# First MLP product of a transformer block on TensorE: plain blocks of features, or seven half-size products per four blocks

## The chip, the cores and the metric

The kernel runs on one core of one Trainium2 chip. The metric is device microseconds of one execution. Matrix products run on TensorE (PE in the profile; PEld is its weight loading), element-wise work on VectorE (DVE), ScalarE (ACT) and GpSimd (POOL). Transfers are issued from queues, mostly SyncE's (SP); those that add onto their destination are issued from GpSimd's queue.

## The reference

One block: a normalization, an input projection, two attention branches, an output projection, and an MLP with a squared ReLU; sequence 512, width 1024, hidden width 4096, all in float32. What the change touches is the MLP line:

```python
    h = h + merged @ w_out[l]
    m = rmsnorm(h, g_mlp[l])
    h = h + jnp.square(jax.nn.relu(m @ w_ff1[l])) @ w_ff2[l]
return rmsnorm(h, g_final)
```

## The kernel before

Every float32 operand is split into a high and a low part, and a product is three matmuls: high by high, high by low, low by high (mm3, lines 87 to 90). A split is one ScalarE pass (the high part) and one VectorE subtraction (split, lines 92 to 94).

The MLP runs in four quarters of eight blocks of 128 hidden features. For each block, hidden loads a weight slice of 1024 x 128 (one DMA of 512 KB), splits it, and multiplies it with the normalized tokens: 8 steps of depth x 3 matmuls = 24 matmuls with 512 tokens as the moving operand. ScalarE evicts the result with a ReLU, and two squares sort its token halves into px and qx. A pair of blocks (pair_units) so gives one 2 x 2 arrangement: rows are token halves, columns are feature blocks.

The second product of a quarter is already done by the seven-product scheme (Strassen-Winograd): the blocks of the second weight, B11 to B22, are combined by add_w2 on VectorE (line 988), the left sides by left_sums on VectorE, and block_product runs seven products of 24 matmuls each, with 512 output columns. prep splits the weights of a product two products ahead; ORDER is the sequence. add_rows (line 1427) adds each result to the rows of h, which live in SBUF to the end. The last products and the final normalization are in last_rows.

Blocks 0 and 1 of the first quarter are multiplied earlier, in two halves of 256 tokens while the rows are still being normalized (early, f00 and f01). The output projection before the MLP uses the same scheme; there load_onto adds pairs of weight blocks by DMA from GpSimd's queue (line 984), and merged_sums forms some left sums on GpSimd.

SBUF tiles come from pools by tag: u2 has 29 buffers of 128 x 512, u4 has 26 of 128 x 2 x 512, wf has 3 weight landings, wh and wl have 4 split weights each. A new tile waits until a buffer of its tag is free. in_program_order pins the order of instructions on chosen engines as they are written; a transfer on SP's queue goes when its buffer is free and its turn comes.

Of the kernel before, what the change touches and what calls it, by code (L numbers as in the profile page):

```python
# [11 lines left out]
F32 = mybir.dt.float32  # L12
# [6 lines left out]
P = 128  # L19
# [37 lines left out]
def tile_block(ctx: ExitStack, tc: tile.TileContext, t, out: bass.AP):  # L57
# [129 lines left out]
    class Flipped:  # L187
        def __init__(self, gains, name):
            self.gains, self.name = gains, name
            self.out = [u4(f"{name}T{k}") for k in range(KD)]  # L190
            self.banks = {}
# [11 lines left out]
        def evacuate(self, half, ks=range(KD)):  # L203
            tok = slice(half * 256, half * 256 + 256)
            for k in ks:
                hl = self.out[k]
                src = self.banks[half][k % 4][:, (k // 4) * 256 : (k // 4) * 256 + 256]
                split_scaled(hl[:, 0, tok], hl[:, 1, tok], src, self.gains[:, k : k + 1])
# [50 lines left out]
    R = one([P, S], F32, "R")  # L259
# [108 lines left out]

    def gated(acc, name):
# [3 lines left out]
        th = u2(f"t{name}")  # L373
        nc.scalar.activation(th, z, AF.Tanh, scale=0.5)  # L374
        return z, th
# [11 lines left out]
    g2 = [gated(f_accs[2 + x], f"b{x}")[1] for x in range(2)]  # L387
# [47 lines left out]
    class Gates:  # L435
# [20 lines left out]
        def sums(self, d):  # L456
            i = 0 if d == "f" else 1
            rr = tl([P, NT, P + 1], F32, "rr", 2, f"rr{d}")
# [469 lines left out]
    def left_sums(px, qx, name, eng):  # L928

        a11, a12, a21, a22 = px[:, 0:HT], px[:, HT:S], qx[:, 0:HT], qx[:, HT:S]  # L930
        y, z = u2(f"y{name}"), u2(f"z{name}")
        s1, s2, s3, s4 = y[:, 0:HT], y[:, HT:S], z[:, 0:HT], z[:, HT:S]
        eng.tensor_tensor(s1, a21, a22, op=ALU.add)
        eng.tensor_tensor(s2, s1, a11, op=ALU.subtract)  # L934
        eng.tensor_tensor(s3, a11, a21, op=ALU.subtract)
        eng.tensor_tensor(s4, a12, s2, op=ALU.subtract)
        return y, z

# [47 lines left out]
    def add_w2(dst, x, y, op):  # L986
        for g in range(NP // 2):
            nc.vector.tensor_tensor(wq[dst][g], wq[x][g], wq[y][g], op=op)  # L988

# [18 lines left out]
    def split_w2(x, name):  # L1008
        return [split_part(x, g, name) for g in range(NP // 2)]

    def merged_sums(p, eng):
        px, qx = merged[p]
        a11, a12, a21, a22 = px[:, 0:HT], px[:, HT:S], qx[:, 0:HT], qx[:, HT:S]
        y, z = u2(f"yo{p}"), u2(f"zo{p}")
# [154 lines left out]
    def finish_zb(f, begun):  # L1171
        g2.append(gated(proj_run(begun, xT), f"b{f}")[1])
# [147 lines left out]
    g2.append(gated(zb, "b6")[1])  # L1320
# [18 lines left out]
    g2.append(gated(proj_run(zb, xT, None, range(3, KD)), "b7")[1])  # L1339
# [108 lines left out]
    def prep(m, qd):  # L1448

        more = qd + 1 < NQ  # L1450
        name = f"b{m}_{qd}"
        if m == 1:
            return split_w2(B11, name)
        if m == 2:
            res = split_w2(B21, name)
            if more:
                load_w2(qd + 1, B21)
            return res
        if m == 3:
            return split_w2(B22, name)  # L1460
        if m == 5:
            add_w2(B11, B12, B11, ALU.subtract)
            return split_w2(B11, name)
        if m == 6:
            add_w2(B11, B22, B11, ALU.subtract)
            return split_w2(B11, name)
        if m == 7:
            add_w2(B12, B22, B12, ALU.subtract)
            res = split_w2(B12, name)
            if more:  # L1470
                load_w2(qd + 1, B12)
                load_w2(qd + 1, B22)
            return res
        add_w2(B11, B21, B11, ALU.subtract)
        res = split_w2(B11, name)
        if more:
            load_w2(qd + 1, B11)
        return res

    def hidden(qd, j):  # L1480

        if qd == 0 and j < 2:
            acc = early[j][2]
# [277 lines left out]
```

## Time and profile before

| | |
|---|---|
| time, median of 3 runs | 759.76 us (759.3 to 759.81) |
| profiled execution | 758.17 us |
| its span, first to last instruction | 756.5 us |
| instructions in the span | 10217 |
| moved by DMA | 81.30 MB, mean 107 GB/s |
| HBM read and written | 76.96 MB, 2.10 MB |

The profiled execution is one run of its own; its span is the time from its first to its last instruction, and what remains lies around it. A row of a group gives line, engine, operation, output and inputs, shapes and count, then busy time and the mean duration of one in ns, then the idle time of the engine just before them. [...]

### The profile page before, as it was taken

How to read it: one execution, taken by the hardware profiler on the slowest of the kernel's cores; microseconds unless marked ns; L12 is line 12 of the kernel's file. 1: busy time of each engine (PE TensorE's matmuls, PEld its weight loads, DVE VectorE, ACT ScalarE, POOL GpSimd, SP SyncE). 2: the span in 40 equal slices, each digit the busy share in tenths (PEclk: the TensorE clock that was granted, in tenths of full speed). 3: DMA queues.
4: the chain of work that ended last, by engine and by line, in shares of the span. 5: the costliest groups of instructions: out<-in, count | busy, mean ns of one | idle time of the engine just before them, and what ended most of it. 6: DMA issues, size and time to landing. Idle time of an engine off the chain costs nothing.

```text
span 756.5 us, 10217 instructions
## 1 busy us (share of the span) xinstructions
PE 745.2 (99%) x3704; PEld 629.7 (83%) x3704; DVE 592.5 (78%) x887; ACT 468.1 (62%) x812; POOL 128.1 (17%) x186
## 2 busy tenths in 40 slices
PE   8999999999999999999999999999999999999996
PEld 7888788888888888899988988888888888888885
DVE  7779899687787787998897787856696578748795
ACT  7556658478767576988866766345544555345644
POOL 1620002031321115036850100000000000000014
PEclk9999999999999999999999999999999999999998
DMA  9832311312234324237998411461126410650003
GB/s 316 255 95 91 128 29 28 84 49 62 59 84 112 60 50 112 73 89 184 273 203 221 133 57 55 139 193 58 56 61 203 127 56 3 206 154 0 29 0 112
DMA packets 97075, 81.30 MB, mean 107 GB/s; under 512 B 15376, under 2 KB 74784, under 8 KB 97024
## 3 DMA queue, kind: packets, MB, share of 16 engines
q1 hardware_dynamic: 93760, 74.07, 33.1%
q0 software_dynamic: 2976, 6.05, 4.3%
q8 instruction: 29, 0.48, 0.3%
q10 hardware_dynamic: 288, 0.52, 0.2%
q14 instruction: 22, 0.18, 0.1%
HBM read 76.96 MB, written 2.10 MB: 105 GB/s over the span
## 4 chain that ended last, share of the span: by engine, by line
PE 93%; ACT 2%; DVE 2%; issue 1%; DMA 1%; POOL 0%; POOLq 0%; ACTq 0%; DVEq 0%
PE f L89 8%; PE f L88 8%; PE f L90 8%; PE gx L88 4%; PE gx L89 4%; PE gx L90 4%; PE first L329 3%; PE tp L1116 2%; PE gz L89 2%; PE gz L88 2%; PE gz L90 2%; PE zb L88 1%; PE za L88 1%; PE zb L90 1%; PE za L90 1%; PE za L89 1%
## 5 line engine op out<-in xcount | busy, mean ns | idle before, releaser
L1700 POOL DMA_DIRECT2D gfin<-in_g_final x1 | 0.6, 623 | 284.1 <-PE f L90 284.1
L988 DVE TENSOR_TENSOR w<-w,w 128x1024 f32<-128x1024 f32 x32 | 38.7, 1219 | 0.3
L1101 ACT ACTIVATE e<-s,top 128x512 f32<-128x512 f32 x32 | 21.9, 685 | 4.4 <-DVE top L1096 3.5
L94 DVE TENSOR_TENSOR pT<-tp,pT 128x512 fp32r<-128x512 f32 x32 | 21.6, 681 | 2.9 <-ACT pT L93 2.9
L1096 DVE TENSOR_REDUCE top<-s 128x1 f32<-128x512 f32 x32 | 21.6, 680 | 2.0 <-PE s L90 1.7
L1427 DVE TENSOR_TENSOR h<-h,gx 128x512 f32<-128x512 f32 x32 | 21.4, 680 | 1.9 <-PE gx L90 1.8
L93 ACT ACTIVATE pT<-tp 128x512 fp32r<-128x512 f32 x32 | 18.8, 592 | 4.3 <-PE tp L1116 4.0
L479 POOL COPY v3f<-rrf 128x4 f32<-128x4 f32 x4 | 2.8, 705 | 109.3 <-DVE rrf L462 109.3
L1116 PE MATMUL tp<-ident,e 128*128 128x128 f32 x128 | 19.3, 274 | 0.3 <-ACT e L1107 0.2
L88 PE MATMUL av<-pT,v 128*128 128x256 f32 x64 | 19.0, 298 | 0.0
L93 ACT ACTIVATE ghb<-y 128x512 fp32r<-128x512 f32 x16 | 10.1, 632 | 14.0 <-DVE y L934 14.0
L1493 ACT ACTIVATE fa<-f 128x512 f32<-128x512 f32 x32 | 18.4, 576 | 0.0
L89 PE MATMUL av<-pT,v 128*128 128x256 f32 x64 | 18.2, 285 | 0.0
L90 PE MATMUL av<-pT,v 128*128 128x256 f32 x64 | 18.2, 284 | 0.0
L1116 PEld LDWEIGHTS tp<-ident,e 128*128 128x128 f32 x128 | 15.1, 140 | 3.7 <-ACT e L1107 1.0
L93 ACT ACTIVATE b_00h<-w 128x1024 fp32r<-128x1024 f32 x7 | 7.4, 1060 | 12.6 <-PE gz L90 6.0
L93 ACT ACTIVATE b_10h<-w 128x1024 fp32r<-128x1024 f32 x7 | 7.4, 1060 | 12.1 <-PE gz L90 6.0
L93 ACT ACTIVATE b_20h<-w 128x1024 fp32r<-128x1024 f32 x7 | 7.4, 1060 | 12.1 <-PE gz L90 6.0
L88 PE MATMUL s<-kbuf,q 96*128 96x512 f32 x32 | 14.1, 441 | 0.0
L374 ACT ACTIVATE tb<-zb 128x512 f32<-128x512 f32 x8 | 5.0, 632 | 14.7 <-DVE zb L372 14.7
L1502 ACT ACTIVATE px<-fa 128x256 f32<-128x256 f32 x32 | 13.4, 418 | 1.0
L984 POOL DMA_DIRECT2D w<-in_w_out x10 | 12.2, 1397 | 6.5 <-DVE bo60l L94 5.3
(1743 smaller groups left out, 2919.1 us busy)
## 6 DMA issues: line engine op xcount, KB each, us to landing
w<-in_w_ff SPq DMA_DIRECT2D x64, 256.0 KB, 3.4
w<-in_w_out POOLq DMA_DIRECT2D x10, 512.0 KB, 8.8
grw<-in_w_in SPq DMA_DIRECT2D x8, 512.0 KB, 9.1
gvw<-in_w_in SPq DMA_DIRECT2D x8, 512.0 KB, 4.5
w<-in_w_out SPq DMA_DIRECT2D x16, 256.0 KB, 5.9
x<-in_xt SPq DMA_DIRECT2D x8, 256.0 KB, 5.3
h<-in_x SPq DMA_DIRECT2D x4, 512.0 KB, 5.1
vw<-in_w_first SPq DMA_DIRECT2D x7, 256.0 KB, 5.4
```

What stands on the lines that cost most here:

```text
L88: nc.tensor.matmul(acc, lh, rh, start=start, stop=False, skip_group_check=onto)
L89: nc.tensor.matmul(acc, lh, rl, start=False, stop=False, skip_group_check=onto)
L90: nc.tensor.matmul(acc, ll, rh, start=False, stop=stop, skip_group_check=onto)
L93: nc.scalar.activation(hi, src, AF.Copy)
L94: rest.tensor_tensor(lo, src, raw(hi), op=ALU.subtract)
L329: nc.tensor.matmul(f_accs[i], a[:, i * P : (i + 1) * P], b, start=k == 0 and x == 0, stop=k == KD - 1 and x == 2)
L988: nc.vector.tensor_tensor(wq[dst][g], wq[x][g], wq[y][g], op=op)
L1096: nc.vector.tensor_reduce(top, acc, axis=AX.X, op=ALU.max, negate=True)
L1101: nc.scalar.activation(e, acc, AF.Exp, bias=top, accum_out=tot[:, qt % 2 : qt % 2 + 1])
L1116: nc.tensor.transpose(tp[:, k * P : (k + 1) * P], e[:, k * P : (k + 1) * P], ident)
L1427: nc.vector.tensor_tensor(hc, hc, acc, op=op)
L1493: nc.scalar.activation(a, acc, AF.Relu)
```

## The change

The first MLP product of blocks 4 to 31 is done by the seven-product scheme too. Four blocks of 128 features form a quad: the weight (1024 x 512) is cut into 2 x 2 blocks of 512 x 256, the normalized tokens into 2 x 2 blocks of depth half by token half. Each of the seven products is 2 feature blocks x 4 steps of depth x 3 = 24 matmuls with 256 tokens. Blocks 0 to 3 stay plain, now all in two token halves. There are seven quads; the first quarter has the four plain blocks and one quad, each later quarter two quads.

- The tokens' sums are formed once (m_sums: two of 128 x 1024 on GpSimd, six on VectorE) and split (m_split, four).
- Each quad needs two weight sums by DMA (load_first, then load_onto from GpSimd's queue) and two by GpSimd (in prep). Five plain loads of 512 KB and two adding ones replace four loads.
- In the second product add_w2 is gone: sums with B12 are adding DMAs, the others GpSimd additions (Group.onto). The left sums (summed_rows) move from VectorE to GpSimd, but for the plain pairs and part of the last.
- Weights are split run by run: a Step is half a second product or one product of a quad, and prepare splits up to two steps ahead; the second product's first steps are interleaved with the last products of the quad before. The order on PE, ScalarE, VectorE and GpSimd is pinned as written.
- u2 goes from 29 to 24 buffers, u4 from 26 to 30; tiles of the early stages (gates, scans, R) change tag.

```diff
-        return tl(list(shape), dt, "u2", 29, name)
+        return tl(list(shape), dt, "u2", 24, name)
-        return tl(list(shape), dt, "u4", 26, name)
+        return tl(list(shape), dt, "u4", 30, name)
...
-    def add_w2(dst, x, y, op):
-        for g in range(NP // 2):
-            nc.vector.tensor_tensor(wq[dst][g], wq[x][g], wq[y][g], op=op)
...
-    def pair_units(qd, p, a22):
-        px, qx = u2(f"px{qd}{p}"), u2(f"qx{qd}{p}")
-        for x in range(2):
-            a = hidden(qd, 2 * p + x)
-            c = slice(x * HT, (x + 1) * HT)
-            nc.scalar.activation(px[:, c], a[:, 0:HT], AF.Square)
-            nc.scalar.activation(qx[:, c], a[:, HT:S], AF.Square)
-        left = {}
-        split_first(left, px, f"{qd}{p}")
-        y, z = left_sums(px, qx, f"{qd}{p}", nc.vector)
-        split_sum(left, y, 5, 6, f"b{qd}{p}")
-        split_sum(left, z, 7, 3, f"c{qd}{p}")
-        split_corner(left, qx, a22, p)
-        return left
...
+    def left_rest(left, p, px, qx, a22, name, eng=nc.gpsimd, low=nc.vector):
+        y, z = summed_rows(px, qx, name, eng)
+        def rest(part=0):
+            if part < 2:
+                split_sum(left, y, 5, 6, f"b{name}", low)
+            if part != 1:
+                split_sum(left, z, 7, 3, f"c{name}", low)
+                split_corner(left, qx, a22, p)
+        return rest
...
+    def m_sums(c):
+        for j in range(2):
+            hi, lo = fm.out[j, c]
+            r = m_raw[j, c] = u4("mr", F32, (P, KD // 2, HT))
+            (nc.vector if c else nc.gpsimd).tensor_tensor(r, raw(hi), raw(lo), op=ALU.add)
+            if j == 0 and c == 1:
+                nc.vector.tensor_tensor(m_raw[0, 0], m_raw[0, 0], r, op=ALU.subtract)
+        if c == 0:
+            return
+        a, b, c, d = (m_raw[k] for k in ((0, 0), (1, 1), (0, 1), (1, 0)))
+        nc.vector.tensor_tensor(c, b, c, op=ALU.subtract)
+        nc.vector.tensor_tensor(b, b, a, op=ALU.add)
+        nc.vector.tensor_tensor(d, b, d, op=ALU.subtract)
+        m_of[1], m_of[2], m_of[3] = fm.out[0, 0], fm.out[1, 0], fm.out[1, 1]
+        m_raw.update({5: a, 6: b, 7: c, 4: d})
...
+    FIRST = (1, 5, 2, 6, 3, 7, 4)
+    class Quad:
+        def __init__(self, q):
+            self.q, self.ready = q, {}
+        def rows(self, i, j):
+            c = (4 * self.q + 2 * i) * P
+            return w1[j * S : (j + 1) * S, c : c + HT].rearrange("(k p) w -> p k w", p=P)
+        def load_first(self):
+            shape = (P, KD // 2, HT)
+            self.a, self.e = (u4(f"w1{x}{self.q}", F32, shape) for x in "ae")
+            for dst in (self.a, self.e):
+                nc.sync.dma_start(dst, self.rows(1, 0))
+        def load_onto(self):
+            for dst, other in ((self.a, (1, 1)), (self.e, (0, 0))):
+                nc.gpsimd.dma_start(dst, self.rows(*other), accum_op=ALU.add)
+        def load_sums(self):
+            self.load_first()
+            self.load_onto()
+        def load(self, x):
+            dst = stage(KD // 2, HT, f"w1{x}{self.q}")
+            nc.sync.dma_start(dst, self.rows(*{"b": (0, 0), "c": (0, 1), "d": (1, 1)}[x]))
+            setattr(self, x, dst)
+        def prep(self, m):
+            src = {1: "b", 5: "a", 2: "c", 6: "b", 3: "c", 7: "e", 4: "d"}[m]
+            wh, wl = halves(KD // 2, HT, f"w1{m}{self.q}")
+            split(wh, wl, getattr(self, src))
+            self.ready[m] = wh, wl
+            if m == 1:
+                nc.gpsimd.tensor_tensor(self.b, self.a, self.b, op=ALU.add)
+            elif m == 2:
+                nc.gpsimd.tensor_tensor(self.c, self.b, self.c, op=ALU.add)
+        def run(self, m):
+            bank = {1: "x", 5: "z", 2: "w", 6: "x", 3: "z", 7: "x", 4: "x"}[m]
+            begin = m in (1, 5, 2)
+            if begin:
+                setattr(self, bank, ps("mm", f"f{bank}{self.q}"))
+            acc = getattr(self, bank)
+            wh, wl = self.ready.pop(m)
+            hi, lo = m_of[m]
+            for x in range(2):
+                c = slice(x * HT, (x + 1) * HT)
+                f = slice(x * P, (x + 1) * P)
+                for k in range(KD // 2):
+                    mm3(acc[:, c], wh[:, k, f], wl[:, k, f], hi[:, k, :], lo[:, k, :],
+                        begin and x == 0 and k == 0, k == KD // 2 - 1, True)
+        def after(self, m):
+            q = self.q
+            if m == 1:
+                self.px = u2(f"px{q}0")
+                nc.scalar.activation(self.px, self.x, AF.Copy)
+            elif m == 5:
+                self.qy = u2(f"qx{q}1")
+                nc.scalar.activation(self.qy, self.z, AF.Copy)
+            elif m == 2:
+                nc.vector.tensor_tensor(self.px, self.w, self.px, op=ALU.add)
+            elif m == 6:
+                self.qx = u2(f"qx{q}0")
+                nc.scalar.activation(self.qx, self.x, AF.Copy)
+            elif m == 3:
+                nc.vector.tensor_tensor(self.qx, self.z, self.qx, op=ALU.add)
+            elif m == 7:
+                nc.vector.tensor_tensor(self.qy, self.x, self.qy, op=ALU.add)
+            else:
+                self.py = u2(f"px{q}1")
+                nc.scalar.activation(self.py, self.x, AF.Relu, scale=-1.0)
+        def chain(self, m, group):
+            q, p = self.q, 2 * (self.q % 2)
+            if m == 2:
+                self.squared(self.px)
+                split_first(group.left[p], self.px, f"{q}0")
+            elif m == 3:
+                self.squared(self.qx)
+                rest = left_rest(group.left[p], p, self.px, self.qx, group.corner(p), f"{q}0")
+                if q == 2 * NQ - 1:
+                    later(do(rest, 1), 4)
+                    later(do(rest, 2), 7)
+                else:
+                    later(rest, 2)
+            elif m == 7:
+                self.squared(self.qy, -1.0)
+                if q == 2 * NQ - 1:
+                    self.y = u2(f"y{q}1")
+                    nc.gpsimd.tensor_tensor(
+                        self.y[:, 0:HT], self.qy[:, 0:HT], self.qy[:, HT:S], op=ALU.subtract
+                    )
+            elif m == 4 and q == 2 * NQ - 1:
+                self.last_pair(group.left[p + 1], group.corner(p + 1))
+            elif m == 4:
+                self.squared(self.py, None)
+                split_first(group.left[p + 1], self.py, f"{q}1")
+                ends = p + 1 == NP - 1
+                rest = left_rest(
+                    group.left[p + 1], p + 1, self.py, self.qy, group.corner(p + 1), f"{q}1",
+                    low=nc.gpsimd if ends else nc.vector,
+                )
+                later(rest, 2, ends)
...
+        def squared(self, x, sign=1.0):
+            if sign is not None:
+                nc.scalar.activation(x, x, AF.Relu, scale=sign)
+            nc.scalar.activation(x, x, AF.Square)
...
+        def onto(self, x, y, g):
+            dst = self.tiles[x, g]
+            if y == B12 and not (self.last and (x, g) == (B11, 1)):
+                nc.gpsimd.dma_start(dst, self.rows(y, g), accum_op=ALU.add)
             else:
+                nc.gpsimd.tensor_tensor(dst, dst, self.tiles[y, g], op=ALU.add)
+        def prep(self, m, g):
+            src = self.tiles[{3: B22, 7: B22, 2: B21}.get(m, B11), g]
+            wh, wl = halves(2, S, f"w2{m}{self.qd}{g}")
+            split(wh, wl, src)
+            self.right.setdefault(m, []).append((wh, wl))
+            if m == 1:
+                self.onto(B11, B12, g)
+            elif m == 5 and g == 1 and self.last:
+                for x in range(2):
+                    self.onto(B11, B22, x)
+            elif m == 3:
+                if not self.last:
+                    self.onto(B11, B22, g)
+                self.onto(B22, B12, g)
+            elif m == 6:
+                self.onto(B11, B21, g)
...
+    w = quads[1]
+    steps = [
+        Step("f02", do(begin_hidden, 2), do(plain_run, 2), do(plain_after, 2), do(plain_chain, 2), [
+            do(w.load, "b"), do(m_sums, 0), w.load_onto, do(m_sums, 1), do(plain_after, 0), do(plain_after, 1),
+            do(w.load, "c"), do(plain_chain, 0), do(plain_chain, 1),
+        ]),
+        Step("f03", do(begin_hidden, 3), do(plain_run, 3), do(plain_after, 3), do(plain_chain, 3), [
+            do(m_split, 5), do(w.load, "d"),
+        ]),
+    ]
+    for qd, g in enumerate(groups):
+        if qd:
+            steps += [quad_step(g, 2 * qd, m) for m in FIRST]
+        odd = {m: quad_step(g, 2 * qd + 1, m) for m in FIRST}
+        if qd:
+            steps.insert(-1, odd.pop(1))
+        steps += [odd[m] for m in FIRST if m in odd]
+        second = 5 if g.last else 2
+        steps[-2:] = [
+            group_step(g, 1, 0), odd[7], group_step(g, 1, 1, (2,)), odd[4],
+            group_step(g, second, 0), group_step(g, 1, 1, (3,)), group_step(g, second, 1),
+        ]
+        for m in (3, 6, 7) if g.last else (5, 3, 6, 7, 4):
+            steps += [group_step(g, m, x) for x in range(2)]
...
+    def prepare(i):
+        while split_so_far[0] < len(wanted):
+            n = split_so_far[0]
+            key = wanted[n]
+            free = n < 2 or (i >= 0 and (n < 4 or final_use[wanted[n - 4]] <= i - 2))
+            next_ = i + 1 < len(steps) and steps[i + 1].needs == key
+            soon = key[0] is not groups[-1] or first_use[key] <= i + {5: 3, 3: 1}.get(key[1], 2)
+            if not next_ and (not free or not soon or key[1:] == (7, 1)):
+                return
+            preps[key]()
+            split_so_far[0] += 1
...
+    for i, step in enumerate(steps):
+        now[0] = i
+        if before and before.after:
+            before.after()
+        step.run()
+        for f in step.hooks:
+            f()
+        for f in due.pop((i, True), []):
+            f()
+        ends = step.needs == (groups[-1], 5, 0)
+        if not ends:
+            prepare(i)
+        if before and before.chain:
+            before.chain()
+        if ends:
+            prepare(i)
+        for f in due.pop((i, False), []):
+            f()
+        before = step
...
+    in_program_order(pinned, PE_ONLY + SPLITTERS + (mybir.EngineType.Pool,))
+    last_rows(g.left, g.right[4], g.right[2], g.xs)
```

More of the change, by code (lines that the diff above doesn't have):

```diff
@@ L1512, in tile_block, with hidden_run, begin_hidden @@
[L1512 to L1514 removed]
+    def hidden_run(begun, half, ks=range(KD)):
+        wh, wl, acc = begun
+        c = slice(half * HT, (half + 1) * HT)
+        for k in ks:
+            hi, lo = fm.out[k // 4, half]
+            mm3(acc[:, c], wh[:, k, :], wl[:, k, :], hi[:, k % 4, :], lo[:, k % 4, :], k == 0, k == KD - 1)
+        return acc
+    def begin_hidden(j):
+        at = traced()
+        early.append(proj_begin(w1, j * P, f"f0{j}"))
+        goes_behind((at, traced()), span["sums"], SP_ONLY)
@@ L1735, in build @@
+    before.after()
+    while split_so_far[0] < len(wanted):
+        preps[wanted[split_so_far[0]]]()
+        split_so_far[0] += 1
+    for x in range(2):
+        g.prep(2, x)
+    in_program_order(pinned, PE_ONLY + SPLITTERS + (mybir.EngineType.Pool,))
+    last_rows(g.left, g.right[4], g.right[2], g.xs)
 def build(arrays):
```

292 lines of the change are left out of this document (177 added, 115 removed).

## The prediction

> **What bounds the kernel now.** I read the page's busy shares first, then the chain that ended last, then the busy time by stretch for the MLP, where the change lies.
>
> ```profile
> PE 745.2 (99%) x3704; PEld 629.7 (83%) x3704; DVE 592.5 (78%) x887; ACT 468.1 (62%) x812; POOL 128.1 (17%) x186
> PE 93%; ACT 2%; DVE 2%; issue 1%; DMA 1%; POOL 0%; POOLq 0%; ACTq 0%; DVEq 0%
> 432.70:746.90 314.20, 314.20 (x1384) 258.82 (x1384) 230.67 (x301) 163.31 (x257) 10.21 (x11) 1.00 0.28 86
> 514.60:596.50 81.90, 81.90 (x362) 67.48 (x361) 58.72 (x76) 40.95 (x62) 0.00 (x0) 1.00 0.34 103
> 746.90:756.50 9.60, 2.91 (x25) 2.70 (x23) 3.83 (x9) 3.69 (x9) 1.72 (x3) 0.80 0.59 219
> ```
>
> The stretch rows give length, then busy time of PE, PEld, DVE, ACT, POOL, the granted clock, the DMA share and GB/s. From 432.7 to 746.9 us (third block of hidden features to the last product) PE has no gap at full clock. VectorE works 73% of that time, ScalarE 52%, GpSimd 3%. So the stage lasts as long as its matmuls take at their pitch, and each matmul saved is time saved while the other engines keep up. The page's 99% alone would not say this, since matmuls overlap; the pitch between starts does.
>
> **The matmuls.** Pitch at N=256 comes from an undisturbed run of starts, pitch at N=512 from the first starts of whole blocks.
>
> ```profile
> 419.40:424.12 4.72, 4.62 (x39) 4.68 (x39) 0.00 (x0) 1.00 0.17 47
> 419.50 0.28 PE L88 MATMUL f<-mT,f00h 128*128 128x256 f32 x1
> 424.05 0.28 PE L90 MATMUL f<-mT,f01l 128*128 128x256 f32 x1
> L88 PE MATMUL f<-mT,f03h x8: 389/389/389, 438.2 to 443.0; 128*128 128x512 f32 x8
> L88 PE MATMUL f<-mT,f06h x8: 389/389/389, 454.5 to 459.3; 128*128 128x512 f32 x8
> ```
>
> 39 matmuls have 38 steps from 419.50 to 424.05: 0.1197 us each, every one with a new weight load, so the loads stay hidden at this size. Blocks 03, 04 and 05 are 72 matmuls from 438.2 to 454.5: 0.2264 each. Two halves thus cost 0.2394, 6% more than one whole, and that eats nearly half of the eighth that seven products of eight save. Four blocks of features cost 96 x 0.2264 = 21.7 us before; a quad costs 7 x 24 = 168 matmuls x 0.1197 = 20.1 us (2.87 per product). Seven quads give -11.3 us. Blocks 02 and 03 stay whole but now run in two token halves: 96 x 0.1197 against 48 x 0.2264, +0.6. The second product has as many matmuls as before. **PE: -10.7 us**, if nothing is late. The last 9.6 us (final rows, stores) are not touched: 0.
>
> **What the other engines do per quad.** Durations overstate what a queue of operations costs; I use start-to-start steps.
>
> ```profile
> 441.03 1.22 DVE L988 TENSOR_TENSOR w<-w,w 128x1024 f32<-128x1024 f32 x1
> 442.16 0.68 DVE L94 TENSOR_TENSOR glc<-z,ghc 128x512 fp32r<-128x512 f32 x1
> 442.77 1.22 DVE L988 TENSOR_TENSOR w<-w,w 128x1024 f32<-128x1024 f32 x1
> 445.96 0.42 DVE L933 TENSOR_TENSOR y<-qx 128x256 f32<-128x256 f32 x1
> 446.30 0.42 DVE L935 TENSOR_TENSOR z<-px,qx 128x256 f32<-128x256 f32 x1
> 443.63 1.06 ACT L93 ACTIVATE b_01h<-w 128x1024 fp32r<-128x1024 f32 x1 [2.10 <-PE f L89]
> 444.60 0.58 ACT L1493 ACTIVATE fa<-f 128x512 f32<-128x512 f32 x1
> 445.83 0.62 ACT L93 ACTIVATE ga<-px 128x512 fp32r<-128x512 f32 x1
> 446.36 0.40 ACT L93 ACTIVATE gd<-qx 128x256 fp32r<-128x256 f32 x1
> L988 DVE TENSOR_TENSOR w<-w,w 128x1024 f32<-128x1024 f32 x32 | 38.7, 1219 | 0.3
> ```
>
> VectorE steps: 1.13 us (1024 columns), 0.61 (512), 0.34 (256). ScalarE: 0.97 (1024), 0.53 (512), 0.58 for an eviction. A quad has seven weight splits instead of four, seven evictions, and the left splits of two pairs. VectorE: 7 x 1.13 + three additions from PSUM at 0.61 + two first splits at 0.61 + two times (2 x 0.61 + 0.34) = 14.1 of 20.1 us. ScalarE: 7 x 0.97 + 4 x 0.58 + 7 ReLU or square passes x 0.53 + 2 x 0.53 + 2 x (2 x 0.53 + 0.33) = 16.7. Neither is the bound by its own work. In the second product VectorE loses the 32 sums of the L988 row (38.7 us); they cost nothing now, being hidden, and gain nothing of themselves. They move to GpSimd and adding DMAs.
>
> ```profile
> 34.81 0.74 POOL L667 TENSOR_TENSOR xz<-x,xy 128x256 f32<-128x256 f32 x1
> 35.51 0.75 POOL L666 TENSOR_TENSOR xz<-x 128x256 f32<-128x256 f32 x1
> 36.20 1.73 POOL L667 TENSOR_TENSOR xz<-x,xy 128x256 f32<-128x256 f32 x1
> 37.90 1.72 POOL L666 TENSOR_TENSOR xz<-x 128x256 f32<-128x256 f32 x1
> 35.96 1.37 DVE L94 TENSOR_TENSOR gr10l<-grw,gr10h 128x1024 fp32r<-128x1024 f32 x1 [1.08 <-ACT gr10h L93]
> 37.26 1.76 DVE L94 TENSOR_TENSOR gr11l<-grw,gr11h 128x1024 fp32r<-128x1024 f32 x1
> 376.38 1.28 POOL L94 TENSOR_TENSOR gao<-mx,gao 128x512 fp32r<-128x512 f32 x1
> 377.62 0.74 POOL L1147 TENSOR_TENSOR mx<-tb,za 128x256 f32<-128x256 f32 x1
> ```
>
> GpSimd steps are 0.70 (256 columns) and 1.24 (512); its 1024-column sum appears nowhere, and two more steps of 0.54 give an estimate of 2.3. The rows from 35.51 on show more: a GpSimd sum beside a VectorE split of two SBUF operands takes 1.7 instead of 0.7, and the next split 1.76 instead of 1.2. They take turns: 1.70 from 36.20 to 37.90 is one split (1.13) and 0.57 of GpSimd. [...]
>
> So I add the two. GpSimd's port time per quad: two weight sums x 2.2, eight pair sums x 0.57 = 9.0; with VectorE's 14.1 that is 23.1 in a quad of 20.1 us. But a pair of quads is interleaved with the next product's first steps (2.72 + 1.36 us of matmuls), and part of its splits falls later: over 14 x 2.87 + 4.1 = 44.3 us I count 16 weight splits (18.1), six additions (3.7), three first splits (1.8), three pair rests (4.7) on VectorE, three weight sums (6.6) and three pairs' sums (6.8) on GpSimd: 41.7 even if nothing overlaps. A split is prepared two products ahead: it starts after the last eviction (0.58), takes 0.97 + 1.13, and is due 5.74 us on: a lead of 3.0 us, more than one GpSimd sum. **Port: 0 in steady state**; bounds 0 and +9.0 (below).
>
> **The adding DMAs.**
>
> ```profile
> DMA to landing us min/median/max: 5.6/8.8/12.3
> 379.00 2.40 POOL L984 DMA_DIRECT2D w<-in_w_out  x2
> f04f<-in_w_ff SPq DMA_DIRECT2D x1, 512.0 KB, 4.0
> q0 software_dynamic: 2351, 4.55, 50.2%
> q1 hardware_dynamic: 5435, 6.92, 39.4%
> 429.80 1.23 DVE L94 TENSOR_TENSOR f03l<-f03f,f03h 128x1024 fp32r<-128x1024 f32 x1 [0.27 <-ACT f03h L93]
> ```
>
> The first row is of the ten adding DMAs of 512 KB in the output product, the queue rows of 348 to 400 us. GpSimd's queue is in order, so an adding DMA waits there for the plain load under it, and the sums behind it wait too. For an odd quad, load 4.0 + two issues 2.4 + landing 8.8 = 15.2, against four products (11.5) and the lead (3.0): 0.7 late, three times. In the second product, split 2.1 + GpSimd sum 2.3 + issue 1.2 + 8.8 = 14.4 against four half products (10.9) and 3.3: 0.2 late, in three quarters. **+2.7 us**; at 5.6 it is 0, at 12.3 it is 23.7. I take the median: the ten landed while both queues together held 90% of the engines, and the new MLP would hold some 60% (4.55 MB at 50.2% of 52 us is 3.0 us per add; eight adds and sixteen plain loads at 1.6 in 78 us).
>
> **The start.** Before the first quad VectorE must form the sums of the normalized features. From the end of f03's split (431.0): six such sums 6.8, two plain pairs 2 x (0.61 + 4 x 0.34) = 3.9, one pair's rest 1.6, eight splits of 1024 columns up to quad 1's fifth product 9.0, two GpSimd weight sums that come between 4.6, and ScalarE's high part before the last split 0.97: 457.9. PE gets there at 432.7 + 11.5 + 4 x 2.87 = 455.7. **+2.2 us**; 0 if VectorE starts earlier or the sums overlap its other work, 6.8 if GpSimd's two feature sums (4.6) fall in the same queue.
>
> **Buffers.** 512-column buffers go from 29 to 24, paired ones from 26 to 30, four gates and two scans move into the latter. Nothing waits for them in the trace that PE feels; 0, bounds -0.5 and +2.
>
> Sum: -10.7 + 2.7 + 2.2 = -5.8. The profiled execution took 758.17 us (span 756.5 and 1.7 around it): 752.4. The median of the runs, 759.76, lies 1.6 above it: **754.0 us**. About 0.2%, 1.5 us, is what a measurement here can tell from no change.
>
> **Rivals.** *The shared port binds each quad by itself* (same or slower): if little of a quad's work slips into the second product, each costs 23.1 instead of 20.1, 7 x 3.0 = 21 less one lead of 3.0 in each of four quarters = 9.0; the sum is -10.7 + 9.0 + 2.7 = +1.0, or 760.8 (757 to 765). For it: the rows at 36 us; against: the 41.7 of 44.3. It decides from 1.5 us per quad on.
>
> *The adding DMAs land late* (slower). With landing L the lateness is 3 x (L - 8.1) + 3 x (L - 8.6) us. At L = 9.8 it takes the 8.5 that are left; at 11.0 it is 15.9, -10.7 + 2.2 + 15.9 = +7.4, or 767.2. For it: the 12.3 maximum and GpSimd's queue holding the sums behind; against: the fuller queues of the rows above.
>
> *Everything hides*: -10.7, or 749.1; the low end of the forecast's own range, 749 to 758.
>
> **How the numbers follow.** Forecast with its range 0.70, port 0.16, late adds 0.14. Faster: nearly all of the first and a little of the second, 0.70. Same: 0.08. Slower: half of the second and nearly all of the third, 0.22. The range goes from 748.6 (all hidden and half a microsecond from the buffers) to 766, leaving out the later half of the late adds.
>
> **What would show it.** PE instructions rise from 3704 to 4256 (7 x 72 + 2 x 24), at a pitch of 0.120 in the new products. The L988 group goes; GpSimd's busy time rises by more than 200 us, with 128x1024 sums of 2.3 us alone and 3.4 beside a split. Waits of PE, none in this stage before, would come at quad 1's fifth product (the split behind the feature sums) and at odd quads' second product. The port rival would show splits of 1.7 or more in most quads with PE waiting for VectorE there; the late adds would show GpSimd and ScalarE waiting for DMA with PE behind them. The forecast is wrong if PE's gaps in the MLP add up to more than 10 us, or if the pitch at N=256 is above 0.125.

## The result: 807.0 us against 759.5, slower by 6%

| | before | after |
|---|---|---|
| median time | 759.5 us (758.2 to 759.8) | 807.0 us (804.3 to 807.8) |
| profiled execution, span | 758.2, 756.5 | 804.3, 802.6 |
| matmuls | 3704 | 4256 |
| block 02 (the third) to the last product but the final rows | 432.7 to 746.9 | 434.7 to 795 |

The ratio is 1.0623, 95% interval 1.0594 to 1.0651. The views below are of the profiled execution, 804.3 us, the shortest of the four. From the page of the changed kernel: the busy shares, the chain that ended last, the group of GpSimd's weight sums and the adding DMAs; the last two rows, from the DMA view of the stage, are the adding DMAs of the quads. A DMA row ends with the median time from issue to landing.

```profile
PE 752.0 (94%) x4256; PEld 653.1 (81%) x4256; DVE 638.5 (80%) x847; ACT 500.3 (62%) x831; POOL 324.7 (40%) x309
PE 66%; DVE 15%; ACT 7%; issue 6%; POOL 3%; DMA 2%; POOLq 0%; DVEq 0%; ACTq 0%; SPq 0%
L1825 POOL TENSOR_TENSOR w<-w,w 128x1024 f32<-128x1024 f32 x9 | 25.6, 2853 | 8.7 <-DVE w2131l L94 5.2
w<-in_w_ff POOLq DMA_DIRECT2D x15, 512.0 KB, 5.8
w1a<-in_w_ff POOLq DMA_DIRECT2D x6, 512.0 KB, 6.8
w1e<-in_w_ff POOLq DMA_DIRECT2D x6, 512.0 KB, 10.2
```

The chain says it shortest: PE held 93% of it before and holds 66% now, and VectorE went from 2% to 15%. By stretch (length, then busy PE, PEld, DVE, ACT, POOL, granted clock, DMA share, GB/s):

```profile
434.70:795.00 360.30, 321.40 (x1952) 282.95 (x1951) 274.82 (x264) 196.48 (x279) 199.12 (x131) 0.97 0.53 127
480.00:490.00 10.00, 9.05 (x39) 7.07 (x39) 8.67 (x8) 6.03 (x8) 7.42 (x5) 1.00 0.29 94
490.00:500.00 10.00, 5.13 (x14) 3.75 (x13) 8.34 (x7) 1.06 (x1) 7.49 (x4) 0.74 0.63 98
```

PE, which had no gap in this stage, now has 39 us of them, and the granted clock is 0.97. The stretch from 490 us shows both at once: 14 matmuls in 10 us where about 44 fit, and 0.74 of the clock.

To see where, I took the starts of all matmuls and set, for each step of the sequence, the time to the next step's first matmul against its matmuls at 0.1197 or 0.2264 us. What is above that is lost. Over the MLP 56.5 us are lost, and 804.3 - 56.5 = 747.8 us is what the changed kernel would take without loss: 10.4 below the 758.2 before. In the same reckoning the kernel before loses 1.6 us, and in its profile the stage begins 1.9 us earlier (432.75 against 434.68), so the matmuls alone make 10.4 + 1.9 - 1.6 = 10.7. So the matmuls saved what they were to save, and the losses are the whole question:

| place | lost, us |
|---|---|
| first quad and the first half products behind it | 6.7 |
| second products of the first three quarters | 25.8 |
| odd quads 3, 5, 7, nearly all at their ends | 9.8 |
| last quarter's second product | 14.0 |
| plain blocks and even quads | 0.2 |

In the even quads the new scheme runs as forecast: the starts of three matmuls of quad 2 are 0.12 us apart, and even a split that lasts 3.12 us instead of 1.2, beside a GpSimd sum, does not hold PE there.

```profile
540.80 0.28 PE L88 MATMUL fx<-mt,w142h 128*128 128x256 f32 x1
540.92 0.28 PE L89 MATMUL fx<-mt,w142h 128*128 128x256 f32 x1
541.04 0.28 PE L90 MATMUL fx<-mt,w142l 128*128 128x256 f32 x1
535.71 3.12 DVE L94 TENSOR_TENSOR w142l<-w1d2f,w142h 128x1024 fp32r<-128x1024 f32 x1
```

The largest loss is in the waits of PE in this stage (sum, times, longest), first row:

```profile
PE gz L88 <- DVE h L1416: 14.6, 3, 4.9
PE fx L88 <- DVE qx L1564: 5.1, 4, 1.7
PE fx L90 <- DVE w161l L94: 3.1, 1, 3.1
```

Three times, once in each of the first three quarters, PE waits 4.9 us between products 5 and 3 for an add_rows (line 1416). The timeline there, VectorE and GpSimd first, then PE:

```profile
485.27 3.32 POOL L1825 TENSOR_TENSOR w<-w,w 128x1024 f32<-128x1024 f32 x1 [1.16 <-DVE w2500l L94]
490.99 2.80 POOL L1825 TENSOR_TENSOR w<-w,w 128x1024 f32<-128x1024 f32 x1
486.25 3.42 DVE L94 TENSOR_TENSOR w2300l<-w,w2300h 128x1024 fp32r<-128x1024 f32 x1
489.59 1.27 DVE L1416 TENSOR_TENSOR h<-h,gw 128x512 f32<-128x512 f32 x2
490.78 4.09 DVE L94 TENSOR_TENSOR w2301l<-w,w2301h 128x1024 fp32r<-128x1024 f32 x1
494.80 1.27 DVE L1416 TENSOR_TENSOR h<-h,gz 128x512 f32<-128x512 f32 x2
490.36 0.39 PE L90 MATMUL gz<-w2501h,glb 128*128 128x512 f32 x1
495.62 0.76 PE L88 MATMUL gz<-w2300h,ghc 128*128 128x512 f32 x1 [4.87 <-DVE h L1416]
497.03 0.63 PE L88 MATMUL gz<-w2300h,ghc 128*128 128x512 f32 x1
497.46 0.63 PE L89 MATMUL gz<-w2300l,ghc 128*128 128x512 f32 x1
```

The two weight splits for product 3 take 3.42 and 4.09 us instead of 1.21, each beside a GpSimd sum, and each ends 1.08 us after that sum (488.59 and 489.67; 493.79 and 494.87). Behind the second, in VectorE's pinned order, stands the add of product 5, which empties the accumulators (banks) gz. Product 3 writes those same banks, so PE stands. When it goes on, matmuls start every 0.43 us instead of 0.23 until about 501.5.

### The profile page after: what moved, and what is told of

Read it like the earlier page. It is cut to its first block, busy times and chain, and to the rows that moved or that the text cites. A ratio compares the mean times of both kernels' runs of the same rounds, so it can differ in the third digit from the quotient of the medians.

```text
span 802.6 us, 11485 instructions
## 1 busy us (share of the span) xinstructions
PE 752.0 (94%) x4256; PEld 653.1 (81%) x4256; DVE 638.5 (80%) x847; ACT 500.3 (62%) x831; POOL 324.7 (40%) x309
## 4 chain that ended last, share of the span: by engine, by line
PE 66%; DVE 15%; ACT 7%; issue 6%; POOL 3%; DMA 2%; POOLq 0%; DVEq 0%; ACTq 0%; SPq 0%
PE first L331 3%; PE gx L88 2%; PE gx L90 2%; PE gx L89 2%; PE tp L1105 2%; PE fx L88 2%; PE fx L90 2%; PE fx L89 2%; PE gz L88 1%; PE zb L88 1%; PE za L88 1%; PE zb L89 1%; PE zb L90 1%; PE za L90 1%; PE za L89 1%
## 5 line engine op out<-in xcount | busy, mean ns | idle before, releaser
L1823 POOL DMA_DIRECT2D w<-in_w_ff x15 | 18.1, 1205 | 50.7 <-DVE w2100l L94 11.1
L1825 POOL TENSOR_TENSOR w<-w,w 128x1024 f32<-128x1024 f32 x9 | 25.6, 2853 | 8.7 <-DVE w2131l L94 5.2
L1416 DVE TENSOR_TENSOR h<-h,gz 128x512 f32<-128x512 f32 x16 | 10.6, 681 | 14.3 <-PE gz L90 14.3
L94 DVE TENSOR_TENSOR ga<-px,ga 128x512 fp32r<-128x512 f32 (+1 forms) x17 | 14.9, 874 | 8.6 <-ACT ga L93 8.6
L94 POOL TENSOR_TENSOR qsf<-qkf,qsf 128x384 fp32r<-128x384 f32 x4 | 4.1, 1015 | 40.0 <-ACT qsf L93 40.0
L1621 ACT ACTIVATE qx<-qx 128x512 f32<-128x512 f32 x14 | 8.9, 634 | 17.8 <-DVE qx L1564 11.2
L1007 POOL TENSOR_TENSOR y<-y,px 128x256 f32<-128x256 f32 x13 | 16.1, 1238 | 7.0 <-ACT px L1622 6.2
L1006 POOL TENSOR_TENSOR y<-qx 128x256 f32<-128x256 f32 x13 | 18.2, 1402 | 0.0
L1136 POOL TENSOR_TENSOR mx<-tb,za 128x256 f32<-128x256 f32 x8 | 6.8, 846 | 25.6 <-DVE tot L1095 23.4
L1621 ACT ACTIVATE px<-px 128x512 f32<-128x512 f32 x7 | 4.4, 635 | 20.3 <-DVE px L1557 20.3
```

Of the source, the lines that this page charges most:

```text
L94: rest.tensor_tensor(lo, src, raw(hi), op=ALU.subtract)
L1006: eng.tensor_tensor(y[:, 0:HT], a21, a22, op=ALU.subtract)
L1416: nc.vector.tensor_tensor(hc, hc, acc, op=op)
L1825: nc.gpsimd.tensor_tensor(dst, dst, self.tiles[y, g], op=ALU.add)
```

## The experiments

Two theories at first. **P**: VectorE's splits and GpSimd's sums take turns, as in the kernel before from 36.20 to 37.90 us (1.70 us for a split of 1.13 and 0.57 of GpSimd), so moving sums to GpSimd delays the splits by whole sums. The prediction and the expectations say shared port for this; that is a name for the turns, and no trace shows a port. **O**: the order makes the wait; product 3 follows product 5 in the same banks without work between (before, the order was 1, 5, 6, 3), so the add of product 5 has no cover. Later came **D** (adding DMAs in a chain land late), and **V** against **L** on what is left at the end. All ratios are to the kernel before, run on the same chip.

### Group sums on VectorE

```diff
-                nc.gpsimd.tensor_tensor(dst, dst, self.tiles[y, g], op=ALU.add)
+                nc.vector.tensor_tensor(dst, dst, self.tiles[y, g], op=ALU.add)
```

> Change of one thing against the changed kernel (807.0 us): the weight sums of the second product that GpSimd adds are added by VectorE instead (16 of 128x1024, adding DMAs stay). Theory P (shared port: GpSimd's long sums stretch VectorE's splits, additions to h stand behind them, PE behind these): the splits of products 3 fall from 3.4 and 4.0 to 1.2 us, the wait of PE ahead of product 3 falls from 4.9 to about 2, in three groups; with the clock that is granted lower after the wait, 807 goes to about 794. Theory O (order: product 3 now follows product 5 in the same PSUM bank, and PE has to wait for the additions that read it): the additions still stand behind the splits prepared ahead, the wait stays at 3 or more and the time at 800 or above.

783.3 us, 1.0329 (1.0314 to 1.0345). VectorE does 17 additions more (not the 16 that the expectation names: twelve in the first three quarters and five in the last, one of these a sum with B12) and PE loses 36.9 us instead of 56.5. The same place:

```profile
487.18 1.27 DVE L1416 TENSOR_TENSOR h<-h,gw 128x512 f32<-128x512 f32 x2
488.38 1.21 DVE L94 TENSOR_TENSOR w2301l<-w,w2301h 128x1024 fp32r<-128x1024 f32 x1
489.51 1.21 DVE L1825 TENSOR_TENSOR w<-w,w 128x1024 f32<-128x1024 f32 x1
490.65 1.27 DVE L1416 TENSOR_TENSOR h<-h,gz 128x512 f32<-128x512 f32 x2
```

The split is back at 1.21 us, the sum costs 1.14 more in VectorE's own queue, and the wait between 5 and 3 is 2.2 us. P holds: the splits and the wait are as it forecast. The time is 10 us better than its 794, which reckoned with product 3 of three quarters alone; in the last quarter, too, the second product loses 8.3 us instead of 14.0. 2.2 us of the wait stay, which O or VectorE's load must explain.

### Product 6 between 5 and 3

```diff
+            elif m == 5 and not self.last:
+                self.onto(B11, B22, g)
             elif m == 3:
-                if not self.last:
-                    self.onto(B11, B22, g)
                 self.onto(B22, B12, g)
-        for m in (3, 6, 7) if g.last else (5, 3, 6, 7, 4):
+        for m in (3, 6, 7) if g.last else (5, 6, 3, 7, 4):
```

> One thing against the changed kernel: in the first three groups the second product runs in the order 1, 2, 5, 6, 3, 7, 4, with product 6 between 5 and 3 (the sum B11 += B22 follows the split for 5). GpSimd keeps its sums. Theory O: PE's waits of 4.9 us ahead of product 3 go, and with them the low clock after them: 3 x about 7 us, so about 786. Theory P: the stretched splits stay and the wait only moves to another product: 799 or above.

823.7 us, 1.0841 (1.0808 to 1.0873): slower than the change itself. The wait ahead of product 3 is gone, as O says, and a larger one has come at product 7. Waits of PE, and the operation of ScalarE it waits for:

```profile
PE gx L88 <- ACT w2710h L93: 7.6, 1, 7.6
PE gx L88 <- ACT w2720h L93: 7.0, 1, 7.0
PE gx L88 <- ACT w2700h L93: 6.8, 1, 6.8
510.04 1.06 ACT L93 ACTIVATE w2700h<-w 128x1024 fp32r<-128x1024 f32 x1 [16.45 <-DMA w<-in_w_ff]
```

The operand of product 7 is B22 + B12, added by a DMA that can be issued only when product 3's split has read B22. With 6 behind 3 that transfer lay under product 6; with 3 directly ahead of 7 nothing covers it. The changed kernel's order had bought cover for the DMA with the cover of the add. As a way to the wait's cause alone this run is confounded.

### Both

> Both of the two edits before. If P and O act in series, the groups after product 2 lose nothing any more: 807 less 3 x about 8.5, about 781. If one alone is the cause, the time is that of the better of the two runs before.

The two edits together: 792.9 us, 1.0448 (1.0428 to 1.0467), slower than either forecast, 781 us or the first run's 783. No wait ahead of product 3 is left, but some 4.4 us a quarter are lost at product 7: PE waits 1.5 us for the high part, whose operand the DMA brings late, 0.8 for the low part, and then matmuls start 0.43 us apart instead of 0.23 (from 506.1 to 509.1 us in the first quarter). The order edit costs 9.6 us on top of the first run. The wait is shorter than in the run before because the transfer lands sooner: here ScalarE starts on it 5.7 us after the issue (503.4 against 497.8). In the run before it took 10.8 (510.0 against 499.2), where two adding DMAs of the next quad were issued from 497.7 on, just ahead of it; here these two went out at 484 us.

### No GpSimd additions in the MLP

The first edit, and the same for the quads' two sums and the pairs' sums and low parts:

```diff
-                nc.gpsimd.tensor_tensor(self.b, self.a, self.b, op=ALU.add)
+                nc.vector.tensor_tensor(self.b, self.a, self.b, op=ALU.add)
...
-    def left_rest(left, p, px, qx, a22, name, eng=nc.gpsimd, low=nc.vector):
+    def left_rest(left, p, px, qx, a22, name, eng=nc.vector, low=nc.vector):
```

> The order of the changed kernel, but all of GpSimd's additions in the MLP (weight sums of the quads and of the second product, sums of pairs, low parts of the last pair in a quarter) go to VectorE; adding DMAs and the two early feature sums stay. Theory P: no split above 1.3 us, the losses at the first quad, at the ends of odd quads and part of those at product 3 go: about 780. Rival: VectorE becomes the bound, 14.1 + 2 x 1.13 + 8 x 0.34 = 19.1 of 20.1 us per quad and additions late everywhere: 805 or above. Theory O alone: about 800, PE still waiting 3 us or more at product 3.

781.1 us, 1.0291 (1.0272 to 1.031): 2.2 us below the first run. PE loses 3.7 instead of 6.7 us at the first quad and 3.9 instead of 9.3 at the odd quads' ends, and more in the second products of the first three quarters (14.7 instead of 12.3), as VectorE now does everything. From 434 us on, 28 of VectorE's operations with 1024 columns took over 1.3 us in the changed kernel, 21 in the first run, and two here.

### The first three quarters' group sums by adding DMA

```diff
-            if y == B12 and not (self.last and (x, g) == (B11, 1)):
+            if not self.last or (y == B12 and (x, g) != (B11, 1)):
                 nc.gpsimd.dma_start(dst, self.rows(y, g), accum_op=ALU.add)
```

B11 + B22 moves behind product 5's split, as in the second run; the order of products stays. These are twelve sums, four per quarter, not the six that the expectation names.

> In the first three groups of feature blocks the six weight sums that GpSimd adds (128x1024) are made by adding DMAs instead, from the weights' rows in HBM; quads, pairs and the last group stay as in the changed kernel. Theory P (GpSimd's 128x1024 sums and VectorE's splits take turns at a shared port, and VectorE's late queue holds the add of product 5): the splits of these groups go back from 3.4 and 4.1 us to about 1.2, VectorE has six sums fewer than in the run with its own sums, and the wait between products 5 and 3 falls from 5.0 us to 1.0 to 2.2 in each group, with no slow matmuls after it: 804.3 - 3 x (3.0 to 4.0) - 6.5 = 786 to 789 us. Theory O (the order of the products alone makes that wait): it stays at 2.2 us or more, 789 us or above. Theory D (three adding DMAs a group in a chain come too late): a PE wait of 5 us or more on a DMA at product 6 or 7 in each group, 800 us or more.

788.4 us, 1.0394 (1.0371 to 1.0417), in P's range. The wait between 5 and 3 is gone altogether (0.0), although the order is as in the changed kernel:

```profile
488.28 1.21 DVE L94 TENSOR_TENSOR w2301l<-w,w2301h 128x1024 fp32r<-128x1024 f32 x1
489.41 0.67 DVE L1416 TENSOR_TENSOR h<-h,gz 128x512 f32<-128x512 f32 x1
490.49 0.69 DVE L1416 TENSOR_TENSOR h<-h,gz 128x512 f32<-128x512 f32 x1 [0.41 <-PE gz L90]
```

The second add of product 5 now waits for PE, and not PE for it. So O is no cause of its own: the banks shared by 5 and 3 cost nothing here, where the splits in VectorE's queue take 1.21 us. D does not appear: what is new, 1.0 to 1.4 us ahead of product 4, is a wait for the add of product 7, not for a transfer.

### The same without GpSimd additions

The last edit and the one before it together.

> As the run before it in this set, and the quads' and pairs' sums and those of the last group are added by VectorE, so that GpSimd adds nothing in the MLP. Theory P: against the run with all sums on VectorE (781.1 us) VectorE is relieved of six sums of about 1.2 us; the 5-to-3 wait of 2.2 us falls to about 1.0: 781.1 - 3 x 1.2 to 3 x 2.2 = 774 to 778 us. Theory O: 781. Theory D: 790 or more.

774.9 us, 1.0213 (1.0196 to 1.0231): in P's range.

### Half of product 2 between 5 and 3

```diff
-            group_step(g, second, 0), group_step(g, 1, 1, (3,)), group_step(g, second, 1),
+            group_step(g, second, 0), group_step(g, 1, 1, (3,)),
         ]
-        for m in (3, 6, 7) if g.last else (5, 3, 6, 7, 4):
+        if not g.last:
+            steps += [group_step(g, 5, 0), group_step(g, 5, 1)]
+        steps += [group_step(g, second, 1)]
+        for m in (3, 6, 7) if g.last else (3, 6, 7, 4):
```

> Only the order: in the first three groups the second half of product 2 (12 matmuls of 0.2264 us, 2.72 us) is moved behind product 5, so that products 5 and 3 have work between them; all sums stay where the changed kernel has them. Theory O: the wait between 5 and 3 falls from 5.0 to 2.3 us and the slow matmuls behind it (2.5, 1.6, 2.5 us) go: 804.3 - 3 x 2.7 - 6.5 = 790 us. Theory P: VectorE is late by its own blocked splits, which the order doesn't shorten; the split for product 3 is itself late, so that the wait comes up ahead of the moved half or behind it: 797 to 804 us.

793.3 us, 1.0454 (1.0438 to 1.0469), between the two. VectorE's splits are as long as before, but 2.72 us of matmuls now lie over them, and there is no wait of 5 us left in these quarters.

```profile
485.08 3.42 DVE L94 TENSOR_TENSOR w2201l<-w221f,w2201h 128x1024 fp32r<-128x1024 f32 x1
490.75 4.15 DVE L94 TENSOR_TENSOR w2301l<-w,w2301h 128x1024 fp32r<-128x1024 f32 x1
```

So cover can stand in for speed: the order decides how much of VectorE's lateness PE feels, and the turns with GpSimd's sums (3.42 and 4.15 us for a split instead of 1.21) make the lateness.

### That and no GpSimd additions, sums by DMA

> Both: no GpSimd additions in the MLP, the first three groups' sums by adding DMAs, and the second half of product 2 between products 5 and 3. If P and O both hold a part, the 5-to-3 wait goes in all three groups: about 3 x 1 to 3 x 2 us below the second run of this set, 769 to 774 us; still above the 758 to 760 us of the kernel before, since the losses at the first quad (about 4 us), at the odd quads' ends (1.6 each) and in the last group (about 9) stand. If only P holds, no further gain: 774 to 778 us.

772.9 us, 1.0187 (1.017 to 1.0204), in the range for both theories. The wait between 5 and 3 was gone already; what the order brought is ahead of product 4, where 0.2 to 0.8 us are lost instead of 0.9 to 1.4. PE loses 24.2 us. The end of an odd quad in this kernel (length, PE, PEld, DVE, ACT, POOL, clock, DMA share, GB/s):

```profile
538.00:566.00 28.00, 25.70 (x158) 22.37 (x157) 24.73 (x38) 19.91 (x30) 4.80 (x4) 1.00 0.80 202
```

VectorE is busy 24.7 of 28 us here, with gaps where it waits for ScalarE's squares and high parts. That suggested the next question: is what is left VectorE's load (V) or the chain eviction, square, split (L)?

### All sums left out

From the last kernel the quads' two sums, the pairs' sums but those of the last pair, and the last quarter's VectorE sums are left out; the splits take the unsummed operands.

```diff
-        y, z = summed_rows(px, qx, name, eng)
+        y, z = px, qx
...
```

> The kernel with no GpSimd additions, the first three groups' sums by adding DMAs and half of product 2 between 5 and 3 (772.9 us, 24 us of PE losses left), with work left out: the two weight sums of each quad, the pairs' sums behind quads and the last group's VectorE sums aren't formed, so the splits take the unsummed operands. Theory V (what is left is VectorE's own load around the change of product): VectorE loses 2 x 1.13 + 8 x 0.34 = 5.0 us per quad, and the losses fall to 8 us or less: 756 us or below. Theory L (what is left is the chain eviction, square, split in the order as pinned, not the load): at most a few us go, 766 us or more.

760.1 us, 1.0011 (1.0001 to 1.0022). Neither theory had it: losses fall from 24.2 to 12.6 us, so the load of these sums is about half of what was left. V is right for the odd quads' ends (3.9 to 0.3) and the first quad (3.7 to 1.0); in the second products (6.8 to 6.4) and the last quarter (9.7 to 4.7) the splits and adds that remain still hold PE. The waits there:

```profile
PE gx L88 <- DVE h L1416: 3.2, 4, 1.2
PE gx L89 <- DVE w2731l L94: 1.6, 1, 1.6
PE gz L89 <- DVE w2521l L94: 0.5, 1, 0.5
```

This run also says how far a better place for these sums could go in this order of products: with them for nothing the kernel only draws level.

### Order 5, 2, 5, 3 by halves

The kernel with losses of 24.2 us, complete, with the second half of product 2 between the halves of 5.

> The same kernel (772.9 us), complete, with the halves in the order 5, 2, 5, 3 in the first three groups, so that the second split of product 5 has 2.72 us more: by theory V the 1.5 us that PE waits for it in each group go, 772.9 - 4.5 = 768.4 us; if VectorE is simply short there, the wait turns up at the next step and the time stays at 771 to 773 us. Either way above the kernel before.

771.2 us, 1.0156 (1.0139 to 1.0173). The 1.5 us went from product 5's second half to product 2's: VectorE is simply short there. Its trace has VectorE without a gap from 475.9 to 487.2 us, and in that stretch PE waits 1.2 us for a low part of product 2. It is the fastest version with the new scheme that I found, 12 us above the kernel before.

### GpSimd additions that nobody needs, and fills

To the run with VectorE's own group sums, 17 GpSimd additions are added that read the split just made and write a buffer that nobody reads; in the second kernel GpSimd fills that buffer with zeros instead.

```diff
-        return tl(list(shape), dt, "u4", 30, name)
+        return tl(list(shape), dt, "u4", 29, name)
...
                 nc.vector.tensor_tensor(dst, dst, self.tiles[y, g], op=ALU.add)
+                nc.gpsimd.tensor_tensor(idle, idle, raw(self.low), op=ALU.add)   # first kernel
+                nc.gpsimd.memset(idle, 0.0)                                      # second kernel
...
```

> The kernel with the group sums on VectorE (783.3 us), to which GpSimd additions of the same size are added in the same places; they write a buffer that nobody reads, and one buffer of the paired kind fewer is left (29). No data hangs on them. Theory P (shared port): VectorE's splits beside them take 3 us and more again although nothing waits for the additions' results: 800 to 812 us. If the lateness in the changed kernel came from waiting for GpSimd's results: 783 to 786 us.

> The same, with GpSimd filling that buffer with zeros (it writes, and reads nothing) in place of adding. Theory P, if the turn-taking is over operands that GpSimd reads: 783 to 786 us, splits of 1.2 us; if writing takes the port too: 795 us or more.

803.2 us, 1.058 (1.0564 to 1.0596), and 784.6 us, 1.0333 (1.0317 to 1.0348). The first is 20 us above the run it is made from, and within 4 us of the change itself; the second is 1 us above it, and level with it by the ratios (1.0333 against 1.0329). First kernel, then second:

```profile
486.25 3.33 POOL L1826 TENSOR_TENSOR idle<-idle,w2300l 128x1024 f32<-128x1024 f32 x1 [3.43 <-DVE w2300l L94]
486.10 1.21 DVE L1825 TENSOR_TENSOR w<-w,w 128x1024 f32<-128x1024 f32 x1
487.23 1.27 DVE L1416 TENSOR_TENSOR h<-h,gw 128x512 f32<-128x512 f32 x2
488.43 2.24 DVE L94 TENSOR_TENSOR w2301l<-w,w2301h 128x1024 fp32r<-128x1024 f32 x1
```
```profile
489.85 1.42 POOL L1826 MEMSET idle<- 128x1024 f32 x1
489.67 1.21 DVE L94 TENSOR_TENSOR w2301l<-w,w2301h 128x1024 fp32r<-128x1024 f32 x1
490.81 1.21 DVE L1825 TENSOR_TENSOR w<-w,w 128x1024 f32<-128x1024 f32 x1
```

Read as turns, the first fence adds up. VectorE's sum has its turn to 487.23, GpSimd's addition then needs 2.35 and ends at 489.58, and the split queued from 488.43 ends at 490.67, 1.09 later. The two adds at 487.23, with one operand in PSUM, ran beside GpSimd at their usual length (1.27 us for the two, as in the run without these additions). Fills of zeros, 0.94 to 1.45 us each, leave the splits at 1.21. VectorE needs none of these GpSimd results, and the trace has no engine waiting for one of these additions. So no dependence costs the 20 us. The additions read two operands in SBUF and the fills read none: 17 of the first cost 20 us, 17 of the second 1 us.

## Why the prediction was wrong

- **PE, -10.7: right.** 4256 matmuls, a pitch of 0.12, and 10.7 us less for the matmuls alone. The L988 group is gone and GpSimd's busy time rose by 197 us, where more than 200 were forecast.
- **Port, "0 in steady state": the step that failed**, by over 20 us. Taking the group sums off GpSimd gave back 19.6 us of losses (56.5 to 36.9), all its additions 24.4 (to 32.1), even though VectorE then had to do them; the upper bound given was 9.0. Three things were missed in it. The 41.7 of 44.3 us was an average over a pair of quads, while the 17 group sums lie in the second products, for which no such count was made: in 480 to 490 us VectorE is busy 8.67 of 10 us and GpSimd 7.42 (the time in which one holds up the other counts as busy). The lead of 3.0 us was held against one sum; two splits follow each other here and each meets one (3.42 + 4.09 - 2 x 1.21 = 5.1 us, the wait of 4.9). And the order was read on GpSimd's side only: what stood behind the blocked split in VectorE's queue, the add that frees product 3's banks, was never named. The rows of the turns, at 36 us, were on the table; the sum was taken at the wrong place. No run shows a port, and the 2.2 us counted for a weight sum was an estimate: the runs showed turns, with such a sum at 2.4 us, or 2.8 to 3.3 beside VectorE's work, and splits of 3.42 and 4.09 us beside it.
- **Cost of a PE wait: missing.** Each of the three long waits is followed by matmuls at 0.43 us; 2.5, 1.6 and 2.5 us go there.
- **VectorE's own load: missing at the changes of product.** The count of 14.1 us of 20.1 per quad was right where quads run alone; at odd quads' ends, in the first half products and in the last quarter VectorE is short without GpSimd too. Leaving its remaining sums out took losses from 24.2 to 12.6 us.
- **Start, +2.2: too small.** 3.4 us at the fourth product of quad 1 and 3.1 in the three half products behind it, with small ones 6.7, near the bound of 6.8 that was put down to GpSimd's two feature sums in the same queue. Without GpSimd's other additions it is 3.7; those two sums stay on GpSimd in that run. The first long wait came at the fourth product, the split for which ended late, and not at the fifth.
- **Adding DMAs, +2.7: not seen.** The second products' landed at 5.8 us (the prediction's low end), the quads' two at 6.8 and 10.2, and no PE wait of the change ends at a DMA. The slow one, w1e, feeds the sixth of a quad's seven products and cost nothing; the one that the second product needs, for which the forecast took 8.8 us, took 6.8. Late landings can cost: in the second run the order took the cover away and PE waited 6.8 to 7.6 us.
- **Rivals.** "The shared port binds" named the right two engines and the wrong place, each quad. Its splits of 1.7 us and more are there in the quads, but the even quads lose nothing. Its price of 9.0 was far too low, and its sum of +1.0 left out the start's 2.2. The waits forecast at odd quads' second product came at their last ones.

Not settled: of the last 12.6 us, how much is order and how much VectorE's splits. And why GpSimd's addition at 490.99 came ahead of the split that had started at 490.78.

## What to carry to other kernels

Before moving two-operand sums from VectorE to GpSimd, look whether they will meet its two-operand work: here a 128x1024 sum of 2.4 us, or 2.8 to 3.3 beside VectorE's work, held a split up for as much as 2.9 us (4.09 against 1.21), so 17 sums of 1.2 us on VectorE were cheaper by some 20 us than on GpSimd. Make the sum of turns at the place where both queues are fullest, for the instruction at the end of the queue, not as an average over the stage. And before saving matmuls on a PE that is 100% busy, ask whether the engine that feeds it has the time: here the scheme drew level only with nearly every sum that was left on VectorE taken out.

## What the runs showed of the hardware

The granted clock fell after some waits of PE. In the changed kernel it fell after each of the three 4.9 us waits (to 0.74, 0.83 and 0.78 in the ten microseconds with the wait or just behind it); with the group sums on VectorE it fell behind a wait of 2.04 us in the second quarter, and not behind the like wait of the first (1.00 from 480 to 500 us). The first row is the stretch around it, with the granted clock of 0.83 behind GpSimd's time:

```profile
575.00:585.00 10.00, 7.96 (x28) 6.29 (x28) 8.49 (x10) 2.50 (x3) 3.87 (x3) 0.83 0.95 159
577.21 0.47 PE L88 MATMUL gz<-w2310h,ghc 128*128 128x512 f32 x1 [2.04 <-DVE h L1416]
579.19 0.63 PE L89 MATMUL gz<-w2310l,ghc 128*128 128x512 f32 x1
579.62 0.63 PE L90 MATMUL gz<-w2310h,glc 128*128 128x512 f32 x1
```

The matmuls there start 0.43 us apart from 578.8 to 581.8, after six at 0.23 to 0.33: a delayed stretch of some 3 us. In the last quarter the longest waits of PE are the same (2.3 and 2.5 us) in the changed kernel and in the run with the first three quarters' sums by adding DMA, whose edit leaves that quarter alone, but 14.0 us are lost there in one and 17.2 in the other; the granted clock was 0.83 in one of the four stretches of ten microseconds from 734 to 774 us in the first, in three of the four from 724 to 764 in the second, and 1.00 in the rest. So, as an estimate from these two figures, a time here carries some 3 us that the schedule does not decide. What decides which waits are followed by a lower clock was not shown.
